# The state-space layer of a decoder trunk: from one scan over 256 tokens to chunks of 8

## The chip, the cores and the metric

One core of a Trainium2 chip runs the whole program. The metric is the device time of one execution in microseconds.

## The reference

Two layers over a residual stream x of 256 tokens by 1024 channels, fp32. Each layer is a gated FFN (1024 to 2816 and back), a mixing step, and a second FFN. The mixing step projects the normalised x by one matrix `w_in` and feeds three mixers: sparse attention (A), a state-space layer (B) and dilated attention (C). Each result goes through its own matrix, is gated by a sigmoid, and the sum goes through `w_out`.

The state-space layer has 32 groups of 16 channels, each with 64 complex states and a diagonal transition:

```
lam_bar = exp(lam * dt);  b_bar = (lam_bar - 1) / lam * b
state[t] = lam_bar * state[t-1] + b_bar @ u[t]
y[t] = Re(c @ state[t]) + d * u[t]
y_b = gelu(y);  y_b = (y_b @ glu_a) * sigmoid(y_b @ glu_b)
```

## The kernel before, in words

Weights are streamed. The list `units` holds them in blocks of 512 KB in the order of use. SP's queue loads each block into one of four buffers `raw` (`load_unit`, line 215); ScalarE rounds it to `wh` (line 226); VectorE, and for a part GpSimd, takes the rest `wl` (lines 230 to 235). Each product is three matmuls in fp32r, high by high and the two cross terms (`mm3`, lines 109 to 111). A block is 24 such matmuls of 256 columns. SP also issues almost every other transfer, in one order.

The Tile framework sets the order on each engine from a simulated timeline and from priorities; `tc.high_priority(offset=-200)` lowers the priority of what is in it.

The FFN (`ffn`, line 341) goes over 11 blocks of 256 hidden channels; in each, VectorE multiplies gate and up, ScalarE rounds (line 375), GpSimd takes the rest (line 376), and the down product follows two blocks later. After each block it calls `side(j)`, into which `step` hangs the set-up of the state-space layer during the first FFN of each layer: `setup_s5_params` once, `setup_s5_layer` one yield at a time, and `setup_s5_table` for each quarter q of the 32 groups.

`setup_s5_table` makes the phase table e^(i theta t) for t = 1 to 256 by eight doublings on GpSimd (lines 493, 495 and 496; VectorE helps at line 494) and stores 1 MB per quarter to DRAM (line 498). `setup_s5_layer` makes the input matrices (to DRAM, as high and low parts) and the output matrices `Cw`, with 16 transposes.

The mixing step is `mix1` (projections, attention, the state-space layer) and `mix2` (GLU, gates, `w_out`). In `mix1` the generator `s5` works on a pair of groups per yield, 16 pairs in a layer. It copies u (high, low, high) into 96 rows of `ub` by twelve small transfers for two pairs (line 825), loads matrix and table (lines 830, 832), multiplies (two matmuls of 256 columns, line 836), turns the product by the table (VectorE line 841, GpSimd 842 and 843), scans the real and the imaginary part over all 256 tokens (line 846), turns back (849 to 851) and multiplies by `Cw` in plain fp32 (line 856). After four pairs come D u and GELU (lines 862 to 870), which leave `yGh` and `yGl` for the GLU.

The order within `mix1` is written by hand: `run(gA, 1)`, `run(gC, n)` and `run(gS, next(steps))` take steps of the attentions and of `s5` between the projections; `SCH` and `steps` say how many for `s5`.

Of the kernel before, what the change touches and what calls it, by code (L numbers as in the profile page):

```python
# [23 lines left out]
F32 = mybir.dt.float32  # L24
# [6 lines left out]
P = 128  # L31
# [11 lines left out]
M_GM, M_CP, M_CN, M_END = 1408, 1410, 1538, 1666  # L43


def const_masks():
# [29 lines left out]
def _body(ctx, tc, nc, I, out, depth, dbg):  # L76
# [119 lines left out]
    YB, VB, MB = 2,4,4  # L196
    DC, BB = V, 1
# [4 lines left out]
    SCH = [1], [2,1,1], [1]  # L202
    TJ = 2
    PO = 100
    TO, TV = -200, 64
# [188 lines left out]
    par = sb([P, 5, 32], F32, "par")  # L394
    smT = sb([P, 16], F32, "smT")
    gqk = sb([P, 4], F32, "gqk")

    def setup_small():
        st = tb([16, P], F32, "st_small")
# [3 lines left out]
        nc.sync.dma_start(st[8:16, :], I["s5_d"].rearrange("l (q g) c -> (l q) (g c)", g=8))  # L403
        pt = ps("y")
        PE.transpose(pt[:, :16], st, ident[:16, :16])
        V.tensor_copy(smT, pt[:, :16])
        V.tensor_tensor(gqk[:, 0:2], smT[:, 0:2], smT[:, 2:4], op=ALU.mult)
        V.tensor_tensor(gqk[:, 2:4], smT[:, 4:6], smT[:, 6:8], op=ALU.mult)

    def setup_s5_params():  # L410
        n = 32
# [23 lines left out]
        V.tensor_copy(im, pt[:, n:2 * n])  # L435
# [4 lines left out]
        r, k = par[:, 0], t("k")  # L440
# [13 lines left out]
        sn, cs = par[:, 4], par[:, 3]  # L454
# [5 lines left out]
        nr, ni, den = t("nr"), t("ni"), t("den")  # L460
        V.tensor_tensor(nr, r, cs, op=ALU.mult)
        V.tensor_scalar(nr, nr, -1.0, None, op0=ALU.add)
# [5 lines left out]
        fr, fi = par[:, 1], par[:, 2]  # L468
# [7 lines left out]
        V.tensor_tensor(fi, fi, den, op=ALU.mult)  # L476

    td = dram.tile([P, 4, 8 * SEQ], F32, name="td", tag="td")
    xd = [dram.tile([P, D], F32, name=f"xd{t}", tag=f"xd{t}") for t in range(2)]
    Bd = [dram.tile([P, 4, 2, P], F32, name=f"Bd{p}", tag=f"Bd{p}") for p in "hl"]  # L480
    Cw = [sb([P, 4, P], F32, f"Cw{i}") for i in range(2)]

    def setup_s5_table(l, q):
        with tc.high_priority(offset=TO):
            tab = tb([P, 4, 2, SEQ], F32, "tab", 1)
            for i in range(2):
                G.tensor_copy(tab[:, :, i, 0], par[:, 3 + i, 16 * l + 4 * q:16 * l + 4 * q + 4])
            n = 1
            while n < SEQ:
                a = tab[:, :, :, 0:n]  # L490
                m = [tb([P, 4, 2, SEQ // 2], F32, f"s5m{i}") for i in range(2)]
                cn, sn = (tab[:, :, i, n - 1:n].unsqueeze(2).broadcast_to([P, 4, 2, n]) for i in range(2))
                G.tensor_tensor(m[0][:, :, :, :n], a, cn, op=ALU.mult)  # L493
                (V if n >= TV else G).tensor_tensor(m[1][:, :, :, :n], a, sn, op=ALU.mult)
                G.tensor_tensor(tab[:, :, 0, n:2 * n], m[0][:, :, 0, :n], m[1][:, :, 1, :n], op=ALU.subtract)  # L495
                G.tensor_tensor(tab[:, :, 1, n:2 * n], m[0][:, :, 1, :n], m[1][:, :, 0, :n], op=ALU.add)  # L496
                n *= 2
            nc.sync.dma_start(td[:, q], tab.rearrange("p j i t -> p (j i t)"))

# [589 lines left out]
```

## Time and profile before

| what | value |
| --- | --- |
| median of 3 runs | 1398.12 us (1396.41 to 1398.65) |
| the profiled execution | 1397.8 us |
| its span, first to last instruction | 1396.0 us |
| mean granted TensorE clock | 0.985 |
| TensorE busy | 1334.4 us, 96% |
| VectorE busy | 948.0 us, 68% |
| ScalarE busy | 670.4 us, 48% |
| GpSimd busy | 639.8 us, 46% |
| DMA | 255.86 MB, mean 183 GB/s |

The busy shares are means over stages that differ: the FFNs, the FFNs with set-up beside them, and the mixing steps. A granted clock of 1 is 2.4 GHz, 0.5 is 1.2 GHz. Matmuls are pipelined: the duration of one record is longer than the distance to the next.

### The profile page before, as it was taken

What the parts mean: (1) busy time and instruction counts of PE and PEld (TensorE: products, weight loads), DVE (VectorE), ACT (ScalarE), POOL (GpSimd) and SP (SyncE); (2) the same over time, 40 slices, a digit from 0 to 9 for tenths busy, and PEclk for the clock granted to TensorE, in tenths of its full rate; (3) what the DMA queues carried; (4) which work ended last, traced back from release to release, by engine and by line L of the source; (5) the groups of instructions that cost most, each with busy time, mean ns of one, the idle gap of its engine ahead of it and who ended that gap; (6) DMA issues with size and microseconds to landing.
All of it is one profiled execution on the core that took longest, in us unless ns stands there. A gap on an engine that the chain in (4) does not pass through costs nothing.

```text
span 1396.0 us, 24668 instructions
## 1 busy us (share of the span) xinstructions
PE 1334.4 (96%) x9624; PEld 1230.7 (88%) x9624; DVE 948.0 (68%) x1256; ACT 670.4 (48%) x962; POOL 639.8 (46%) x670
## 2 busy tenths in 40 slices
PE   8998999988999999999999989999899999999998
PEld 7987899977789989999998889899787899899997
DVE  5656666999997475444667565579999955744443
ACT  5442355656454545444543334466655545544442
POOL 0678705476667441111178751165766765211110
PEclk9999999999999999999999999999999999999999
DMA  8755587555446656666755667755544475466662
GB/s 260 229 181 170 183 273 221 154 151 151 139 132 201 191 175 196 182 182 185 233 164 185 215 207 227 232 176 155 166 141 131 139 222 186 133 213 184 186 190 91
DMA packets 210388, 255.86 MB, mean 183 GB/s; under 512 B 22552, under 2 KB 190560, under 8 KB 209248
## 3 DMA queue, kind: packets, MB, share of 16 engines
q1 hardware_dynamic: 209552, 251.67, 59.1%
q10 hardware_dynamic: 720, 2.62, 0.5%
q8 instruction: 75, 1.23, 0.4%
q14 instruction: 41, 0.34, 0.1%
HBM read 237.48 MB, written 13.63 MB: 180 GB/s over the span
## 4 chain that ended last, share of the span: by engine, by line
PE 60%; POOL 16%; DVE 13%; DMA 6%; issue 4%; ACT 1%; SPq 0%; POOLq 0%; ACTq 0%; DVEq 0%
PE mm L111 14%; PE mm L110 14%; PE mm L109 14%; POOL s5m L493 4%; POOL tab L495 3%; DVE wl L233 3%; POOL tab L496 2%; DMA td<-tab 2%; PE pt L110 2%; PE pt L111 2%; PE pt L109 2%; PE sc L111 2%; PE sc L110 2%; PE sc L109 2%; DMA raw<-in_ffn_gate_dram 2%
## 5 line engine op out<-in xcount | busy, mean ns | idle before, releaser
L233 DVE TENSOR_TENSOR wl<-raw,wh 128x1024 fp32r<-128x1024 f32 (+3 forms) x376 | 487.5, 1304 | 266.6 <-ACT wh L226 263.5
L226 ACT ACTIVATE wh<-raw 128x1024 fp32r<-128x1024 f32 (+2 forms) x396 | 413.1, 1047 | 436.7 <-PE mm L110 197.4
L111 PE MATMUL mm<-hTh,wl 128*128 128x256 f32 x1728 | 495.3, 287 | 12.8 <-DVE wl L233 12.7
L110 PE MATMUL mm<-hTl,wh 128*128 128x256 f32 x1728 | 492.7, 285 | 0.0
L109 PE MATMUL mm<-hTh,wh 128*128 128x256 f32 x1728 | 492.6, 285 | 0.0
L111 PEld LDWEIGHTS mm<-hTh,wl 128*128 128x128 f32 x1728 | 329.2, 191 | 17.5 <-DVE wl L233 14.9
L109 PEld LDWEIGHTS mm<-hTh,wh 128*128 128x128 f32 x1728 | 330.1, 191 | 4.1 <-issue 3.2
L110 PEld LDWEIGHTS mm<-hTl,wh 128*128 128x128 f32 x1728 | 328.8, 190 | 4.6 <-issue 3.6
L376 POOL TENSOR_TENSOR al<-aa,ah 128x512 fp32r<-128x512 f32 x40 | 71.6, 1791 | 427.7 <-ACT ah L375 409.9
L235 POOL TENSOR_TENSOR wl<-raw,wh 128x384 fp32r<-128x384 f32 (+2 forms) x108 | 135.5, 1260 | 34.9 <-ACT wh L226 31.0
L109 PE MATMUL mm<-wh,hTh 128*128 128x256 f32 (+1 forms) x496 | 142.4, 289 | 1.1 <-DVE yGl L710 0.9
L110 PE MATMUL mm<-wl,hTh 128*128 128x256 f32 (+1 forms) x496 | 142.3, 289 | 0.0
L111 PE MATMUL mm<-wh,hTl 128*128 128x256 f32 (+1 forms) x496 | 140.3, 287 | 0.0
L110 PEld LDWEIGHTS mm<-wl,hTh 128*128 128x128 f32 x496 | 94.0, 190 | 3.1 <-issue 2.5
L109 PEld LDWEIGHTS mm<-wh,hTh 128*128 128x128 f32 x496 | 94.1, 190 | 2.9 <-PE mm L111 1.2
L111 PEld LDWEIGHTS mm<-wh,hTl 128*128 128x128 f32 x496 | 93.3, 190 | 1.5 <-issue 0.8
L230 POOL TENSOR_TENSOR wl<-raw,wh 128x512 fp32r<-128x512 f32 x40 | 56.6, 1435 | 49.5 <-ACT wh L226 49.5
L846 DVE TENSOR_TENSOR_SCAN v<-par,v 128x256 f32<-128x256 f32 x64 | 61.8, 971 | 3.7 <-POOL v L842 3.5
L110 PE MATMUL pt<-wl,ah 128*128 128x512 f32 x144 | 57.1, 397 | 5.7 <-DVE wl L233 5.7
L493 POOL TENSOR_TENSOR s5m<-tab 128x8 f32<-128x8 f32 (+3 forms) x64 | 55.8, 872 | 4.7
L850 POOL TENSOR_TENSOR v<-M 128x256 f32<-128x256 f32 x32 | 26.0, 812 | 68.7 <-DVE M L849 61.0
L111 PE MATMUL pt<-wh,al 128*128 128x512 f32 x144 | 56.7, 393 | 0.0
(288 smaller groups left out, 2288.5 us busy)
## 6 DMA issues: line engine op xcount, KB each, us to landing
raw<-in_w_in_dram SPq DMA_DIRECT2D x100, 512.0 KB
raw<-in_ffn_gate_dram SPq DMA_DIRECT2D x88, 512.0 KB
raw<-in_ffn_up_dram SPq DMA_DIRECT2D x88, 512.0 KB
raw<-in_ffn_down_dram SPq DMA_DIRECT2D x88, 512.0 KB
td<-tab SPq DMA_DIRECT2D x8, 1024.0 KB
tab<-td SPq DMA_DIRECT2D x16, 512.0 KB
raw<-in_w_out_dram SPq DMA_DIRECT2D x16, 512.0 KB
raw<-in_w_branch_a_dram SPq DMA_DIRECT2D x8, 512.0 KB
```

The source lines that it names most:

```text
L109: PE.matmul(o, lh, rh, start=start, stop=False)
L110: PE.matmul(o, lh, rl, start=False, stop=False)
L111: PE.matmul(o, ll, rh, start=False, stop=stop)
L226: A.activation(hv, r, AF.Copy)
L230: G.tensor_tensor(lv[:, :, cs], r[:, :, cs], hv[:, :, cs].bitcast(F32), op=ALU.subtract)
L233: V.tensor_tensor(lv[:, :, :c], r[:, :, :c], hv[:, :, :c].bitcast(F32), op=ALU.subtract)
L235: G.tensor_tensor(lv[:, :, c:], r[:, :, c:], hv[:, :, c:].bitcast(F32), op=ALU.subtract)
L376: G.tensor_tensor(al, a, ah.bitcast(F32), op=ALU.subtract)
L493: G.tensor_tensor(m[0][:, :, :, :n], a, cn, op=ALU.mult)
L495: G.tensor_tensor(tab[:, :, 0, n:2 * n], m[0][:, :, 0, :n], m[1][:, :, 1, :n], op=ALU.subtract)
L496: G.tensor_tensor(tab[:, :, 1, n:2 * n], m[0][:, :, 1, :n], m[1][:, :, 0, :n], op=ALU.add)
L846: V.tensor_tensor_scan(v[:, i], rr, v[:, i], 0.0, op0=ALU.mult, op1=ALU.add)
```

## The change

The state-space layer is reformulated by chunks of 8 tokens (32 chunks). Within a chunk the output is a lower triangular block Toeplitz matrix of 8 x 16 by 8 x 16 per group, times the chunk's 128 inputs; a second 128x128 matrix takes the inputs to the state at the chunk's end, a third takes the state before the chunk to the outputs. States of 64 complex numbers lie as 128 partitions (real and imaginary halves). Only the step between chunks is scanned: 32 steps for each of the 8 groups of a quarter, all in one instruction of 256 elements, whose factor is zero where a group begins.

Set-up: `setup_s5_params` keeps lam_bar and its second and fourth power, the phase of the eighth, and its modulus. `setup_s5_layer` makes eight powers `Qt` on VectorE, one phase table of 32 steps for all groups on GpSimd, and per quarter the matrices F (GpSimd) and H (VectorE), 128x1024 each. F is transposed (8 transposes) and stored to `Ad`; H is stored to `Gd`; the Toeplitz blocks are 16 short matmuls of F by H, stored to `Kd`. All of it is inside the lowered priority.

Run time: u is stored to DRAM with its tokens reversed in each chunk, and read back with (channel, token) on the partitions; the result goes to DRAM in the same way and comes back as `yGh` and `yGl`, whose tokens are then ordered by place in the chunk first. The GLU's last two steps in `mix2` write them back to token order by a strided view. All matmuls of the new layer are in plain fp32: per quarter 8 in `enter` and 16 in `leave`, with 32 columns each.

```diff
-    SCH = [1], [2,1,1], [1]
...
-    def setup_s5_table(l, q):
...
-            while n < SEQ:
...
-            nc.sync.dma_start(td[:, q], tab.rearrange("p j i t -> p (j i t)"))
...
+        for i, nme in enumerate(("s5_b_re", "s5_b_im")):
+            nc.sync.dma_start(b[0][64 * i:64 * i + 64], I[nme][l].rearrange("g p c -> p g c"))
+            nc.sync.dma_start(b[1][64 - 64 * i:128 - 64 * i], b[0][64 * i:64 * i + 64])
...
+        Qt = tb([P, 2, 2, 32, 8], F32, "s5Q")
...
+        while n < 32:
+            mm = [a[:, :64 * n].rearrange("p (a g n) -> p a g n", a=2, n=n) for a in m]
             for i in range(2):
+                G.tensor_tensor(mm[i], tab[:, :, :, :n], tab[:, i, :, n - 1:n].unsqueeze(1).broadcast_to([P, 2, 32, n]), op=ALU.mult)
+            G.tensor_tensor(tab[:, 0, :, n:2 * n], mm[0][:, 0], mm[1][:, 1], op=ALU.subtract)
+            G.tensor_tensor(tab[:, 1, :, n:2 * n], mm[0][:, 1], mm[1][:, 0], op=ALU.add)
+            n *= 2
...
+        for i, a in enumerate((tab[:, 0], tab[:, 1], R)):
+            nc.sync.dma_start(td[:, :, i, :], a.rearrange("p (q g) k -> p q (g k)", q=4))
...
+        for q in range(4):
+            gs = slice(8 * q, 8 * q + 8)
+            F, m1 = xt(0), xt(1)
+            f4, m4 = (a.rearrange("p (g c n) -> p g c n", g=8, n=8) for a in (F, m1))
+            for i, o in enumerate((f4, m4)):
+                G.tensor_tensor(o, b[i][:, gs].unsqueeze(3).broadcast_to([P, 8, 16, 8]),
+                                Qt[:, i, 1, gs].unsqueeze(2).broadcast_to([P, 8, 16, 8]), op=ALU.mult)
+            G.tensor_tensor(F, F, m1, op=ALU.add)
+            H, m2 = xt(0), xt(1)
...
+            V.tensor_tensor(H, H, m2, op=ALU.add)
+            nc.sync.dma_start(Gd[:, q], H)
             yield
+            At = xt(1)
+            for hf in range(2):
+                pt = ps("y")
+                for g in range(4):
+                    k = 4 * hf + g
+                    PE.transpose(pt[:, g * P:(g + 1) * P], F[:, k * P:(k + 1) * P], ident)
+                A.activation(At[:, 512 * hf:512 * hf + 512], pt, AF.Copy)
+            nc.sync.dma_start(Ad[:, q], At)
+            pk = ps("y")
+            for s in range(2):
+                for part in range(2):
+                    for a in range(4):
+                        g = 4 * s + a
+                        o = pk[32 * a:32 * a + 32, 128 * s:128 * s + 128]
+                        lh = F[:, (g - a % 2) * P:(g - a % 2 + 2) * P:8]
+                        if part:
+                            PE.matmul(o[:, 16:], lh, h4[:, g, 0:7].rearrange("p n c -> p (n c)"), start=True, stop=True)
...
+            for a in range(4):
+                nc.sync.dma_start(Kd.rearrange("(s a) x n c -> a x s (n c)", a=4)[a][:, 2 * q:2 * q + 2, 112:],
...
-            A.activation(uh, pu, AF.Copy)
-            V.tensor_tensor(ul, pu, uh.bitcast(F32), op=ALU.subtract)
+            uv = tb([P, 512], F32, "M", MB).rearrange("p (c t) -> p c t", c=2)
+            A.activation(uv.rearrange("p c (r k) -> p c r k", r=8), pu.rearrange("p c (k r) -> p c r k", r=8)[:, :, ::-1, :], AF.Copy)
+            nc.sync.dma_start(ud[2 * b:2 * b + 2].rearrange("q p t -> p q t"), uv)
...
+            def late(q):
+                Gt, Tt = tb([P, 8, 128], F32, "s5G"), tb([P, 8, 128], F32, "s5T")
+                nc.sync.dma_start(Gt.rearrange("p g e -> p (g e)"), Gd[:, q])
+                kq = Kd[8 * q:8 * q + 8]
+                for r in range(8):
+                    nc.sync.dma_start(Tt[r::8], kq[:, :, r:r + 8, :].rearrange("g x n c -> x g (n c)"))
...
+            def enter(q):
+                At = sb([P, 1024], F32, "x0")
+                nc.sync.dma_start(At, Ad[:, q])
+                tab = tb([P, 3, 256], F32, "tab")
+                nc.sync.dma_start(tab, td[:, q])
+                U = tb([P, 8, 32], F32, "s5U", 2)
+                nc.sync.dma_start(U, ud[q].rearrange("(g c) (r k) -> (c r) g k", c=16, r=8))
+                bu = ps("p2")
+                for g in range(8):
+                    PE.matmul(bu[:, 32 * g:32 * g + 32], At[:, P * g:P * g + P], U[:, g], start=True, stop=True)
+                X = bu[:, :256]
+                sw = tb([P, 256], F32, "s5sw")
+                for e in range(2):
+                    A.activation(sw[hps[e]], X[hps[1 - e]], AF.Copy)
+                v, w = tb([P, 256], F32, "s5v", 2), tb([P, 256], F32, "s5w", 2)
+                V.tensor_tensor(v, X, tab[:, 0], op=ALU.mult)
+                V.tensor_tensor(w, sw, tab[:, 1], op=ALU.mult)
+                V.tensor_tensor(v, v, w, op=ALU.subtract)
+                V.tensor_tensor_scan(v, tab[:, 2], v, 0.0, op0=ALU.mult, op1=ALU.add)
...
+            def leave(q, Gt, Tt):
+                U, v = st.pop(q)
                 yT = ps("y")
+                for g in range(8):
+                    PE.matmul(yT[:, 32 * g:32 * g + 32], Tt[:, g], U[:, g], start=g == 0, stop=False)
+                for g in range(8):
+                    PE.matmul(yT[:, 32 * g + 1:32 * g + 32], Gt[:, g], v[:, 32 * g:32 * g + 31], start=False, stop=g == 7)
...
+                for r in range(8):
+                    nc.sync.dma_start(yd[q].rearrange("i (g c) (r k) -> r c (i g) k", c=16, r=8)[r],
+                                      yo[16 * r:16 * r + 16].bitcast(F32).rearrange("p i (g k) -> p (i g) k", k=32))
+
+            def back(q):
+                for i, a in enumerate((yGh, yGl)):
+                    nc.sync.dma_start(a[:, q].bitcast(F32), yd[q, i])
...
+        steps = iter([1, 0, 1, 0, 1, 0] + [1, 0, 1] + [1, 0, 1, 0, 1, 0, 1, 0] + [1] * 4)
```

## Rows read from the trace of the kernel before

**Rows 1.** The page, part 1: busy us, share of the span, instructions.

```profile
PE 1334.4 (96%) x9624; PEld 1230.7 (88%) x9624; DVE 948.0 (68%) x1256; ACT 670.4 (48%) x962; POOL 639.8 (46%) x670
```

**Rows 2.** Windows by stage: us, busy us of each engine (instructions), clock, DMA share, GB/s.

```profile
15.00:222.40 207.40, 197.33 (x1348) 183.13 (x1347) 132.40 (x145) 87.70 (x105) 113.52 (x151) 0.97 0.69 214
222.40:517.70 295.30, 278.19 (x2112) 252.19 (x2111) 248.08 (x412) 161.38 (x273) 188.24 (x169) 0.99 0.56 167
517.70:706.50 188.80, 188.80 (x1342) 178.04 (x1342) 97.44 (x94) 86.76 (x102) 19.21 (x12) 1.00 0.63 189
706.50:909.10 202.60, 194.01 (x1357) 181.59 (x1356) 126.17 (x107) 85.65 (x103) 110.63 (x150) 0.98 0.65 206
909.10:1205.20 296.10, 278.94 (x2112) 253.13 (x2111) 248.92 (x411) 161.63 (x273) 188.23 (x169) 0.99 0.55 167
1205.20:1393.00 187.80, 187.09 (x1326) 176.04 (x1324) 88.78 (x84) 78.55 (x89) 18.14 (x11) 1.00 0.54 164
```

**Rows 3.** Windows within the mixing stage of layer 0, columns as above.

```profile
245.00:280.00 35.00, 33.96 (x284) 33.51 (x283) 34.39 (x98) 22.80 (x44) 16.83 (x15) 1.00 0.54 151
280.00:315.00 35.00, 28.92 (x218) 25.34 (x217) 34.65 (x57) 20.44 (x40) 27.39 (x25) 1.00 0.51 147
240.00:445.00 205.00, 189.41 (x1495) 169.04 (x1494) 194.37 (x349) 114.28 (x209) 137.48 (x130) 0.98 0.52 152
```

**Rows 4.** Groups by line, 240 to 445 us: count, busy us, mean ns, idle before.

```profile
L846 DVE TENSOR_TENSOR_SCAN v<-par,v 128x256 f32<-128x256 f32 x32 | 30.5, 959 | 1.8 <-POOL v L842 1.7
...
L849 DVE TENSOR_TENSOR M<-v,tab 128x512 f32<-128x512 f32 x32 | 23.3, 768 | 0.1
L841 DVE TENSOR_TENSOR M<-p,tab 128x512 f32<-128x512 f32 x32 | 20.9, 680 | 0.2
...
L634 ACT ACTIVATE cq<-pt 64x512 fp32r<-64x512 f32 x6 | 3.5, 588 | 11.2 <-DVE cq L635 11.2
...
L740 DVE TENSOR_TENSOR yAl<-pt,yAh 128x256 fp32r<-128x256 f32 x2 | 0.8, 408 | 0.0
```

**Rows 5.** Groups by line on PE, mixing stage of layer 0, columns as above.

```profile
L109 PE MATMUL mm<-hTh,wh 128*128 128x256 f32 x224 | 64.2, 287 | 0.0
...
L856 PE MATMUL y<-v,Cw 128*32 128x256 f32 x64 | 15.8, 414 | 7.3 <-POOL v L850 7.3
...
L836 PE MATMUL p<-x,bs 96*128 96x256 f32 x32 | 7.4, 313 | 3.0 <-issue 3.0
```

**Rows 6.** Timeline of PE and its weight loads: start, duration, what, count.

```profile
358.20 0.28 PE L109 MATMUL mm<-hTh,wh 128*128 128x256 f32 x1
358.32 0.28 PE L110 MATMUL mm<-hTl,wh 128*128 128x256 f32 x1
...
360.31 0.28 PE L774 MATMUL sc<-ck,cq 128*128 128x128 f32 x1
360.42 0.28 PE L775 MATMUL sc<-ckl,cq 128*128 128x128 f32 x1
...
400.87 1.53 PE L788 MATMUL pt<-att_pt,cv 128*64 128x128 f32 x24
...
402.33 0.20 PEld L734 LDWEIGHTS pt<-ident,att_s 128*128 128x128 f32 x2 [0.17 <-ACT att_s L722]
```

**Rows 7.** Groups by line, 705 to 925 us, the set-up's and the FFN's.

```profile
L376 POOL TENSOR_TENSOR al<-aa,ah 128x512 fp32r<-128x512 f32 x10 | 18.1, 1806 | 65.8 <-ACT ah L375 48.0 <-DMA raw<-in_w_in_dram 17.8
...
L493 POOL TENSOR_TENSOR s5m<-tab 128x1024 f32<-128x1024 f32 x4 | 11.8, 2944 | 0.3
...
L494 DVE TENSOR_TENSOR s5m<-tab 128x1024 f32<-128x1024 f32 x4 | 4.9, 1226 | 4.0 <-POOL tab L496 4.0
```

**Rows 8.** The chain that ended last, near 84 us: start, us, what.

```profile
84.41 7.82 DMA td<-tab
```

**Rows 9.** Line 825's issues on SP: ns min/median/max, first and last start.

```profile
L825 SPq DMA_DIRECT2D x<-yGh x64: 507/581/1439, 255.3 to 1076.1; - x64
```

**Rows 10.** The page, part 3: queue, packets, MB, share of 16 engines.

```profile
q1 hardware_dynamic: 209552, 251.67, 59.1%
```

More of the change, by code (lines that the diff above doesn't have):

```diff
@@ L402, in setup_small @@
                 nc.sync.dma_start(st[2 * i:2 * i + 2, 64 * hf:64 * hf + 64], I[nme])
-        nc.sync.dma_start(st[8:16, :], I["s5_d"].rearrange("l (q g) c -> (l q) (g c)", g=8))
         pt = ps("y")
-        PE.transpose(pt[:, :16], st, ident[:16, :16])
-        V.tensor_copy(smT, pt[:, :16])
+        PE.transpose(pt[:, :8], st, ident[:8, :8])
+        V.tensor_copy(smT, pt[:, :8])
+        for i in range(2):
+            V.tensor_tensor(sgn[:, i:i + 1], cm[:, M_GM + 1 - i:M_GM + 2 - i], cm[:, M_GM + i:M_GM + i + 1], op=ALU.subtract)
         V.tensor_tensor(gqk[:, 0:2], smT[:, 0:2], smT[:, 2:4], op=ALU.mult)
@@ L459, in setup_s5_params @@
         A.activation(cs, k, AF.Sin)
[L460 to L462 removed]
+        nr, den = t("nr"), t("den")
+        ni = zs[:, 0, 1, 0]
+        V.tensor_tensor(zs[:, 0, 0, 0], r, cs, op=ALU.mult)
+        V.tensor_scalar(nr, zs[:, 0, 0, 0], -1.0, None, op0=ALU.add)
         V.tensor_tensor(ni, r, sn, op=ALU.mult)
@@ new lines, in setup_s5_params @@
+        sq = tb([P, 2, 2, n], F32, "sp_sq")
+        for i in range(3):
+            a, b = zs[:, i], zs[:, i + 1]
+            V.tensor_tensor(sq, a, a, op=ALU.mult)
+            V.tensor_tensor(b[:, 0], sq[:, 0], sq[:, 1], op=ALU.subtract)
+            V.scalar_tensor_tensor(b[:, 1], a[:, 0], 2.0, a[:, 1], op0=ALU.mult, op1=ALU.mult)
+        V.tensor_copy(lam, zs[:, 0:3, :, 0])
+        V.tensor_copy(u8, zs[:, 3, :, 1])
+        V.tensor_tensor(r8, r, r, op=ALU.mult)
+        V.tensor_tensor(r8, r8, r8, op=ALU.mult)
@@ new lines, in s5 @@
+            st = {}
+            def late(q):
[4 more added lines that the diff above has]
+                    nc.sync.dma_start(Tt[r::8], kq[:, :, r:r + 8, :].rearrange("g x n c -> x g (n c)"))
+                return Gt, Tt
+            def enter(q):
[17 more added lines that the diff above has]
+                V.tensor_tensor_scan(v, tab[:, 2], v, 0.0, op0=ALU.mult, op1=ALU.add)
+                sw = tb([P, 256], F32, "s5sw")
+                for e in range(2):
+                    A.activation(sw[hps[e]], v[hps[1 - e]], AF.Copy)
+                V.tensor_tensor(v, v, tab[:, 0], op=ALU.mult)
+                V.tensor_tensor(w, sw, tab[:, 1], op=ALU.mult)
+                V.tensor_tensor(v, v, w, op=ALU.add)
+                st[q] = U, v
@@ L873, in run @@
+            GT = late(0)
+            for q in range(5):
+                if q < 4:
+                    enter(q)
+                    yield
+                if q > 0:
+                    leave(q - 1, *GT)
+                    if q < 4:
+                        GT = late(q)
+                    if q > 1:
+                        back(q - 2)
+                    yield
+            back(3)
         def run(gen, n=None):
@@ L884, in mix1 @@
         gS = s5()
-        steps = iter([v for a, k in zip(SCH, (6, 3, 8)) for v in (a * k)[:k]] + [1] * 4)
+        steps = iter([1, 0, 1, 0, 1, 0] + [1, 0, 1] + [1, 0, 1, 0, 1, 0, 1, 0] + [1] * 4)
         for g in range(3):
@@ L1007, in f @@
                         setup_s5_params()
-                next(gen, None)
-                if j % TJ == 0 and (j - 2) // TJ < 4:
-                    setup_s5_table(l, (j - 2) // TJ)
+                with tc.high_priority(offset=TO):
+                    next(gen, None)
         return f
```

234 lines of the change are left out of this document (98 added, 136 removed).

## The prediction, made before the changed kernel was built or run

> **What bounds the kernel now.** I read the page's busy shares first, then a table by stage, then the stretch that differs. TensorE is busy for 1334 of 1396 us [rows 1], so the time can fall only by TensorE's idle time, by its half-speed stretches, or by work taken off it. The stage table [rows 2] cuts the span at the last update of x in each stage (line 329). The second FFN of layer 0 shows the pace of weights alone: 188.8 us, no idle time, full clock. The FFN of layer 1 with the state-space set-up beside it takes 202.6 us, 13.8 more for the same weights. The two mixing stages take 295.3 and 296.1 us; TensorE is busy for 278.2 of the first, so 17.1 us are idle, and the granted clock of 0.99 says that some of it ran at 1.2 and not 2.4 GHz. A mean of 0.99 costs about 1% of the stage, 3 us.
>
> Why TensorE idles there shows in the slices [rows 3]: from 245 to 315 us VectorE is busy for 34.4 and 34.7 of every 35 us while TensorE drops to 28.9. VectorE is full, and everything TensorE waits for (the transposed operands, the softmax minima) stands in its line. So VectorE sets the pace of that stretch and TensorE the rest.
>
> **What leaves VectorE.** One layer's rows [rows 4]: 32 scans of 256 (30.5 us), 32 products after them (23.3) and 32 before them (20.9), together 74.7 us of VectorE's 194.4 in that stretch. The new code has 4 chunks, each with one scan of the same 256 elements (0.96 us) and six products or sums of 128x256. The nearest row for such a one is the 128x256 subtract, 0.41 us: 0.96 + 6 x 0.41 = 3.4 us, 13.7 per layer. GELU's steps change little (two additions with D go, one product comes from GpSimd) and I leave them even. Net 61 us per layer leave an engine that had 10 us to spare; it then has about 133 us of work in 205. All of GpSimd's additions on v go too. ScalarE gets four half-partition copies per chunk, at most 0.59 us each (line 634 copies twice the width [rows 4]), some 9 us in a stage where it is busy for 161 of 295 [rows 2]; covered.
>
> **What changes on TensorE in a mixing stage.** Out go 64 output products (15.8 us) and 32 input products (7.4): 23.2 us, and with them 7.3 + 3.0 us of idle time right before them [rows 5]. In come 24 matmuls a chunk, 96 a layer: plain fp32, a full 128x128 stationary block, 32 moving columns. The trace has none like it, so bounds. Below: 24 matmuls of line 788 (fp32, half-width weights, in pairs) in 1.53 us, 0.064 each. Above: 0.41 us, the whole duration of an fp32 matmul of 256 columns at line 856, as if nothing overlapped. Between them lie 4-byte 128x128 weights under 128 columns, which start 0.11 us apart at lines 774 and 775 [rows 6]; the weights, not the columns, must set that pace, since 256 columns start 0.12 us apart. Plain fp32 may load worse, so I take 0.14: 96 x 0.14 = 13.4 us.
>
> Of the old idle time and lost clock, 17.1 + 3.0 = 20.1 us, I let 5 us stay: waits on the attention's own chains (normalise, transpose, softmax), which are late next. Gain per mixing stage: 23.2 + 15.1 - 13.4 = 24.9 us, two layers 49.8.
>
> A rule that speaks against this: the Trainium skill, "FP8 and Floating Point Precision", TensorE Precision Notes, counts four passes through the array for true fp32. The trace neither proves nor excludes it here: the fp32 matmul of line 856 lasts 0.414 us where a one-pass one of the same 256 columns lasts 0.287 [rows 5], more than one pass and less than four. If weights were loaded for each pass, the price would go to the upper bound; that is a rival below.
>
> **The set-up, beside the first FFN of each layer.** Out go the tables: 8 doubling steps per quarter on GpSimd, the longest 2.9 us an instruction, between which the FFN's own 1.8 us subtract (line 376) has to stand in line, and a table store whose landing (7.82 us) holds GpSimd's next table [rows 7, 8]. In come one table of 32 steps (the same kinds of instruction, five doublings, no second table waiting for a store) and per quarter three GpSimd and three VectorE operations on 128x1024. On VectorE these cost 12 x 1.23 = 15 us per layer, plus about 6 for the eight powers, less 4.9 or more of its share in the tables [rows 7]; it is busy for 126 of 202.6 us [rows 2], so they are covered. What is not covered is TensorE's: 24 transposes more (40 for 16; the pair at 402.33 loads in 0.20, so 0.10 each [rows 6]: 2.4 us) and 64 short matmuls for the Toeplitz blocks at 0.064 (4.1 us): 6.5 us per layer. Against it stand the old stalls: 13.8 us in layer 1, and in layer 0 10.1 idle plus 3% of clock (6.2): 16.3. I let 5 us of stalls stay in each, because the two transposed halves and the Toeplitz blocks of each quarter pass one after the other through the one PSUM bank "y": twelve hand-overs from TensorE to ScalarE and back per layer. Gain: 13.8 - 11.5 = 2.3 and 16.3 - 11.5 = 4.8, together 7.1.
>
> **DMAs and the queue of SP.** Each mixing stage issues 90 transfers for this layer in place of 80, the set-up 40 in place of 14. At the 0.58 us of the old small copies [rows 9] that is 21 us more of SP's time over 500 us; SP mostly waits for a free weight buffer, so nothing. By the row of q1 [rows 10] a packet takes 0.591 x 16 x 1396 / 209552 = 63 ns on average, at 1.2 KB. The new layouts move 24,600 runs of 128 bytes; at no less than nothing and at most 63 ns each they add up to 97 us of all 16 engines over two stages of 591, from a share of 0.55 to 0.71 [rows 2]. Hidden either way. What matters is the order: SP also issues the weight loads, and a load that reads what a store wrote waits in SP for the landing. Four weight buffers of 24 matmuls at 0.12 us (lines 109 and 110 [rows 6]) are 11.5 us of cover.
>
> The strided copies (u reversed, the merge back to token order) have no row; nothing below, and above as much again as a 128x256 operation, 8 x 0.41 = 3 us in all, under other matmuls. I take nothing.
>
> **Sum.** 49.8 + 7.1 = 56.9 us off the profiled 1397.8 (span 1396.0 and 1.8 around it; the median of the runs is 1398.12, the same): **1341 us**.
>
> **Rivals.**
> 1. Everything waiting goes and the short matmuls run at 0.064: mix 23.2 + 20.1 - 6.1 = 37.2 each, set-up 30.1 - 13 = 17.1, together 91.5: 1306 us. For it: VectorE is the only full engine. Against: softmax chains need TensorE, VectorE and ScalarE in turn.
> 2. The old waits before the state-space matmuls come back as waits for their loads (u and y go out to DRAM and return): 10.3 us a stage stay beside the 5, and the set-up gains nothing. 23.2 + 4.8 - 13.4 = 14.6 a stage: 1369 us. For it: TensorE takes its work in order, and the 3.0 us before line 836 were already of that kind.
> 3. The 192 short matmuls of both layers cost 0.41 each: 192 x 0.27 = 52 us more than in the sum, 1393 us. That is what the four passes of the Trainium skill (same section) would come to if each pass also reloads the weights.
> 4. **Slower: SP blocks the weights.** A chunk has two places where a load waits for a store (u, y), 8 a layer. If each holds SP for two landings in a row as long as the table store's, 2 x 7.82 = 15.6 us, the 11.5 us of weight buffers run dry and TensorE stands still for 4.1 us, 16 times: 66 us, 1407 us. It decides from holds of 11.5 + 56.9/16 = 15 us. For it: one queue for everything. Against: that store is 1 MB, and the new ones are 256 KB.
>
> **How the numbers follow.** Chances: forecast 0.51 (1326 to 1356), rival 1 0.15, rival 2 0.17, rival 3 0.07, rival 4 0.10. A measurement of this kernel tells 0.2%, about 3 us. Forecast and rivals 1 and 2 are faster, rival 3 by a hair and with half its chance surely: 0.86 faster, 0.03 the same, 0.11 slower. The range goes from a little under rival 1 to just short of rival 3: 1297 to 1390; what is left out is most of rivals 3 and 4 and a little below.
>
> **What would show each step.** Right: scans at 8 and not 64, VectorE at 70 to 80% in the mixing stages and below 90% in every slice from 245 to 385; mixing stages of 265 to 275 us; the 192 short matmuls starting 0.10 to 0.16 us apart; the FFN with set-up within 12 us of the one without. Wrong: TensorE idle before the short matmuls with a DMA as releaser (rival 2), starts 0.3 us or more apart (rival 3), weight conversions on ScalarE waiting for a raw load in the mixing stage (rival 4), or clock levels of 0.9 where it is 1.0 now.

## The result, and the profile of the changed kernel

The changed kernel takes 1364.13 us (median of 4 runs, 1362.91 to 1365.29) where the kernel before, on the same chip, takes 1398.38: a ratio of 0.9756 with an interval of 0.9739 to 0.9772. It is faster, as forecast, and inside the range; but it gained 34 us where 57 were forecast.

The page's busy shares and the row of SP's queue, against [rows 1] and [rows 10]:

```profile
PE 1333.8 (98%) x10120; PEld 1257.6 (92%) x10120; DVE 842.1 (62%) x1166; ACT 700.7 (51%) x1018; POOL 474.4 (35%) x333
...
q1 hardware_dynamic: 245488, 261.44, 64.0%
```

TensorE is busy for as long as before (1334 us): what went is idle time, and the matmuls taken out were replaced by as much work. VectorE lost 106 us, GpSimd 165.

The table by stage, cut as in [rows 2] (us, busy us of PE, PEld, DVE, ACT and POOL with their instructions, clock, DMA share, GB/s):

```profile
15.00:219.00 204.00, 198.89 (x1501) 183.25 (x1500) 153.71 (x180) 94.84 (x117) 91.69 (x50) 1.00 0.73 224
219.00:504.50 285.50, 277.96 (x2207) 266.66 (x2206) 177.01 (x337) 169.37 (x289) 132.45 (x101) 0.98 0.64 186
504.50:693.20 188.70, 188.70 (x1342) 177.98 (x1341) 97.27 (x94) 86.89 (x102) 19.21 (x12) 1.00 0.64 188
693.20:893.50 200.30, 197.53 (x1508) 184.21 (x1507) 140.67 (x126) 92.82 (x115) 77.63 (x49) 1.00 0.68 214
893.50:1171.70 278.20, 273.40 (x2209) 262.62 (x2208) 178.40 (x339) 169.50 (x289) 133.04 (x101) 1.00 0.65 191
```

Beside [rows 2]: the FFNs with set-up went from 207.4 to 204.0 and from 202.6 to 200.3, the FFN without set-up stands at 188.7. The mixing stages went from 295.3 to 285.5 and from 296.1 to 278.2: 9.8 and 17.9 us, where the forecast had 24.9 for each. The two layers run the same code and differ by 7.3 us; that is the first question. Why even the better one is 7 us short is the second.

The matmul groups of the mixing stage of layer 0, against [rows 5]:

```profile
L900 PE MATMUL p<-s5U,x 128*128 128x32 f32 x64 | 9.4, 304 | 2.5 <-DMA s5U<-ud 2.5
...
L922 PE MATMUL y<-s5U,s5T 128*128 128x32 f32 x64 | 8.1, 268 | 0.0
L924 PE MATMUL y<-s5v,s5G 128*128 128x31 f32 x64 | 7.8, 275 | 0.0
...
L637 PE MATMUL pt<-ident,qn 128*128 128x128 f32 x32 | 5.3, 283 | 2.9 <-DVE qn L633 2.9
```

The code issues 32 matmuls on each of lines 900, 922 and 924 (4 chunks of 8). The trace has 64 of each. A plain fp32 matmul is two records, each with its own weight load: 192 in the stage, not 96. The timeline of PE gives their pace:

```profile
297.65 1.42 PE L922 MATMUL y<-s5U,s5T 128*128 128x32 f32 x12
298.90 1.95 PE L924 MATMUL y<-s5v,s5G 128*128 128x31 f32 x16
300.69 0.37 PE L106 MATMUL mm<-wh,hTh 128*128 128x256 f32 x1
...
352.50 3.62 PE L900 MATMUL p<-s5U,x 128*128 128x32 f32 x16 [2.49 <-DMA s5U<-ud]
```

Sixteen records of line 924 stand between 298.90 and 300.69: 0.112 us each, close to the 0.11 and 0.12 us of 128x128 weights under 128 and 256 columns [rows 6]. The last row is as many records of line 900 at 352.50, after a wait of 2.49 us for the load of u; the next matmul starts at 355.94, so these take 0.215 us each. Windows around both places, columns as in the stage table:

```profile
297.00:301.00 4.00, 4.00 (x37) 3.98 (x37) 3.09 (x7) 2.90 (x5) 2.83 (x2) 1.00 0.78 248
301.00:304.40 3.40, 3.40 (x18) 3.07 (x16) 3.25 (x6) 0.64 (x2) 0.33 (x2) 0.50 0.53 142
304.40:308.00 3.60, 3.60 (x31) 3.29 (x32) 2.88 (x12) 2.29 (x6) 1.53 (x1) 1.00 0.97 310
350.00:352.50 2.50, 0.01 (x1) 0.00 (x0) 1.91 (x4) 1.53 (x5) 1.00 (x1) 0.93 0.52 85
352.50:359.00 6.50, 6.50 (x30) 6.50 (x31) 1.45 (x4) 1.26 (x3) 0.00 (x0) 0.50 0.86 280
```

The granted clock is 0.50, that is 1.2 GHz, in two stretches of 9.9 us together. A short record takes 0.215 us there and 0.112 at 2.4 GHz; if all the work in them slows down alike, half of the time is lost, an estimate of 5.0 us. One follows the wait for u. The other follows the short matmuls, with TensorE busy for all of the 4 us ahead of it. The chain of waits around the wait for u (start, us, what):

```profile
342.13 5.43 DMA s5G<-Gd
...
347.93 0.45 SPq L936
...
349.93 2.53 DMA s5U<-ud
...
352.50 3.62 PE p L900 x16
```

The load of u is issued by SP behind the y stores (line 936), which in this chain follow the load of G. SP's own rows show that its order differs between the layers (first two rows layer 0, last two the same quarter in layer 1):

```profile
345.27 4.61 SPq L936 DMA_DIRECT2D yd<-s5y  x8
349.93 0.46 SPq L897 DMA_DIRECT2D s5U<-ud  x1
...
1018.13 0.59 SPq L897 DMA_DIRECT2D s5U<-ud  x1
1018.82 5.18 SPq L936 DMA_DIRECT2D yd<-s5y  x8
```

In layer 1 the load stands ahead of the stores, and TensorE does not wait for it.

Last the slices, against [rows 3]:

```profile
240.00:275.00 35.00, 32.96 (x275) 32.15 (x274) 33.55 (x103) 23.44 (x48) 14.79 (x14) 1.00 0.65 185
275.00:310.00 35.00, 34.08 (x278) 32.84 (x278) 31.36 (x64) 27.93 (x60) 17.85 (x14) 0.95 0.67 192
310.00:345.00 35.00, 35.00 (x304) 33.41 (x302) 22.40 (x44) 26.03 (x48) 12.71 (x9) 1.00 0.63 181
```

VectorE is still full in the first 35 us (the attention's own work and 7.9 us of weight rests; the state-space lines 906 to 909 take 1.9), and by the third slice it has room (22.4 of 35). The DMAs carry 36,000 packets more, and TensorE waits for none of them but that one load of u.

### The profile page after: what moved, and what is told of

The parts are those of the page before. It is cut to its first block, busy times and chain, and to the rows that moved or that the text cites. A ratio compares the mean times of both kernels' runs of the same rounds, so it can differ in the third digit from the quotient of the medians.

```text
span 1362.7 us, 25418 instructions
## 1 busy us (share of the span) xinstructions
PE 1333.8 (98%) x10120; PEld 1257.6 (92%) x10120; DVE 842.1 (62%) x1166; ACT 700.7 (51%) x1018; POOL 474.4 (35%) x333
## 4 chain that ended last, share of the span: by engine, by line
PE 76%; DVE 8%; DMA 6%; POOL 5%; ACT 2%; issue 2%; SPq 1%; POOLq 0%; ACTq 0%; DVEq 0%
PE mm L108 18%; PE mm L106 17%; PE mm L107 17%; DVE wl L228 3%; PE pt L108 3%; PE pt L107 3%; PE pt L106 3%; PE sc L108 2%; PE sc L107 2%; PE sc L106 2%; DMA raw<-in_w_in_dram 2%; DMA raw<-in_ffn_gate_dram 1%; ACT wh L221 1%; DMA raw<-in_ffn_down_dram 1%; PE p L900 1%
## 5 line engine op out<-in xcount | busy, mean ns | idle before, releaser
L228 DVE TENSOR_TENSOR wl<-raw,wh 128x1024 fp32r<-128x1024 f32 (+3 forms) x376 | 471.8, 1262 | 338.2 <-ACT wh L221 334.0
L106 PEld LDWEIGHTS mm<-hTh,wh 128*128 128x128 f32 x1728 | 326.6, 189 | 2.2
L107 PEld LDWEIGHTS mm<-hTl,wh 128*128 128x128 f32 x1728 | 325.2, 188 | 1.6 <-issue 0.3
L371 POOL TENSOR_TENSOR al<-aa,ah 128x512 fp32r<-128x512 f32 x40 | 68.2, 1706 | 466.1 <-ACT ah L370 466.1
L230 POOL TENSOR_TENSOR wl<-raw,wh 128x384 fp32r<-128x384 f32 (+2 forms) x108 | 144.9, 1347 | 199.6 <-ACT wh L221 166.9
L108 PE MATMUL sc<-wh,al 128*128 128x512 f32 x144 | 56.5, 392 | 0.0
L106 PE MATMUL pt<-wh,ah 128*128 128x512 f32 x144 | 56.4, 392 | 0.0
L107 PE MATMUL sc<-wl,ah 128*128 128x512 f32 x144 | 56.3, 391 | 0.0
```

The costliest lines, as they stand in the source:

```text
L106: PE.matmul(o, lh, rh, start=start, stop=False)
L107: PE.matmul(o, lh, rl, start=False, stop=False)
L108: PE.matmul(o, ll, rh, start=False, stop=stop)
L228: V.tensor_tensor(lv[:, :, :c], r[:, :, :c], hv[:, :, :c].bitcast(F32), op=ALU.subtract)
L230: G.tensor_tensor(lv[:, :, c:], r[:, :, c:], hv[:, :, c:].bitcast(F32), op=ALU.subtract)
L371: G.tensor_tensor(al, a, ah.bitcast(F32), op=ALU.subtract)
```

## The experiments

The theory after the result: VectorE's line did set the old pace and no longer does; what is missing is the doubled count of short matmuls, and in layer 0 the wait for u with the slow clock behind it. The edits below are against the changed kernel, except three that are against the kernel before. Stage times are those of the one profiled execution of each run.

**The short matmuls in fp32r.** A, T and u are declared as the reduced-precision type of four bytes; G stays plain.

```diff
-                At = sb([P, 1024], F32, "x0")
+                At = sb([P, 1024], F32R, "x0")
...
-                U = tb([P, 8, 32], F32, "s5U", 2)
+                U = tb([P, 8, 32], F32R, "s5U", 2)
...
-                Gt, Tt = tb([P, 8, 128], F32, "s5G"), tb([P, 8, 128], F32, "s5T")
+                Gt, Tt = tb([P, 8, 128], F32, "s5G"), tb([P, 8, 128], F32R, "s5T")
```

> Blocks A and T and the input u of the state-space layer are declared fp32r in place of plain fp32, so these products run in reduced precision; the products with G stay plain fp32. Theory (the miss is the price of plain fp32: the trace of after has two records per matmul, 0.112 us apart, so 192 and not 96 per layer): lines 900 and 922 fall from 128 to 64 records each, their distance stays near 0.11 us, 64 x 0.112 = 7.2 us per mixing stage, 14 us in all: about 1350 us. Rival (the short matmuls wait in the shadow of other stalls, or fp32r loads cost twice as much): under 4 us, 1360 or more.

Measured: 1355.48 us (1354.33 to 1358.52), ratio 0.9696 (0.9668 to 0.9724). Its PE groups in the mixing stage of layer 0, and its two mixing stages:

```profile
L924 PE MATMUL y<-s5v,s5G 128*128 128x31 f32 x64 | 9.4, 293 | 0.0
L637 PE MATMUL pt<-ident,qn 128*128 128x128 f32 x32 | 5.3, 283 | 4.6 <-DVE qn L633 4.6
L922 PE MATMUL y<-s5U,s5T 128*128 128x32 f32 x32 | 4.4, 255 | 0.0
L900 PE MATMUL p<-s5U,x 128*128 128x32 f32 x32 | 4.1, 256 | 0.0
```

```profile
220.70:496.90 276.20, 269.22 (x2144) 258.83 (x2143) 181.06 (x339) 168.80 (x289) 132.03 (x101) 0.99 0.67 192
...
885.80:1161.30 275.50, 269.20 (x2144) 258.80 (x2143) 182.61 (x339) 168.95 (x289) 132.69 (x101) 0.99 0.67 193
```

The records of lines 900 and 922 halve, those of line 924, left plain, don't: the type sets the count. The gain is 8.6 us, less than the 14 expected and more than the rival's 4. Part of the time came back as waits for the normalised q (line 637 waits 4.6 us and not 2.9) and as clock (0.99 in layer 1, where it was 1.00). The 9.3 us of layer 0 are not the price of the records alone, since its wait for u is gone too; in layer 1, which had no such wait, 64 records fewer took 4.2 us off TensorE's busy time and 2.7 off the stage.

**u from another queue.** The load of u is issued by ScalarE's queue.

```diff
-                nc.sync.dma_start(U, ud[q].rearrange("(g c) (r k) -> (c r) g k", c=16, r=8))
+                nc.scalar.dma_start(U, ud[q].rearrange("(g c) (r k) -> (c r) g k", c=16, r=8))
```

> Only the load of u (256 KB per quarter) is issued from ScalarE's queue and not from SP's. Theory (in layer 0 TensorE waits 2.5 us for this load, which stood in SP behind nine loads of G and T and eight stores of y; the wait drops TensorE's clock for 6.8 us, 3.4 us lost): the wait and the 1.2 GHz stretch behind it go, the mixing stage of layer 0 falls by 5 to 7 us to about 279, layer 1 stays at 278: about 1358 us. Rival (the order of ScalarE is disturbed by the waits of the issue, or the next load in SP is late instead): mixing stage of layer 0 at 284 to 287, no gain or a loss of a few us.

Measured: 1361.69 us (1361.08 to 1362.64), ratio 0.9734 (0.9712 to 0.9756). The two mixing stages, and two windows between:

```profile
221.70:500.20 278.50, 274.39 (x2211) 264.37 (x2210) 178.43 (x338) 169.42 (x289) 131.94 (x101) 0.99 0.66 190
...
890.00:1169.70 279.70, 274.44 (x2208) 264.03 (x2207) 179.71 (x339) 169.32 (x289) 133.01 (x101) 0.99 0.66 190
...
266.40:269.90 3.50, 3.50 (x35) 3.50 (x33) 3.43 (x15) 3.31 (x4) 0.65 (x2) 1.00 0.71 186
269.90:273.30 3.40, 3.40 (x18) 3.40 (x18) 3.33 (x18) 1.61 (x8) 0.75 (x1) 0.50 0.61 172
```

Layer 0 loses its wait and 7.0 us, nearly all that set it apart from layer 1. But layer 1 takes 1.5 us more, and the two FFNs with set-up 3.5, at clocks of 0.98 to 0.99 where they were 1.00. The last two rows show one such stretch, in layer 0, with TensorE busy throughout. So the total falls by 2.4 us and not by 6, and the intervals of the two ratios overlap (0.9712 to 0.9756 and 0.9739 to 0.9772).

**The floor.** The run-time part of the state-space layer is left out (no loads, matmuls, scans, GELU), and u goes straight to the GLU; the set-up stays.

```diff
-        gS = s5()
+        gS = iter(range(8))
```

> Leaves out the run-time part of the state-space layer: u goes straight to the GLU, no loads, no short matmuls, no scan; the set-up stays. It gives the floor of a mixing stage. Theory (in layer 1 nothing but the 192 records of 0.112 us is left of the layer's cost): the mixing stages fall from 285 and 278 to 256 to 258 us each. Rival (the attention's chains share waits with it, so more goes than TensorE's own time): 245 to 252. Rival (the layer runs in gaps that stay without it): 265 or more.

Measured: 1321.28 us (one run). The mixing stages:

```profile
219.30:480.00 260.70, 254.59 (x2016) 243.42 (x2015) 164.51 (x296) 157.15 (x261) 136.47 (x101) 0.99 0.55 161
...
869.10:1128.70 259.60, 254.17 (x2016) 243.34 (x2015) 164.74 (x296) 157.33 (x261) 136.31 (x101) 0.99 0.55 162
```

The floor keeps 5.4 to 6.1 us idle. The old layer cost 34.6 and 36.5 us above it, the new one 24.8 and 18.6; 192 records at 0.112 are 21.5. In layer 1 TensorE's busy time falls by 19.2 us (273.4 to 254.2), and the floor has a stretch of 3.4 us at 1.2 GHz in each stage, by estimate 1.7 us of lost clock, which explains most of what is missing to 21.5. The stages lie 1.6 to 2.7 us above the theory's 256 to 258; neither rival came.

**VectorE filled up again.** 160 products of 128x240 a stage that nobody reads.

```diff
+            def load(n):
+                for i in range(n):
+                    V.tensor_tensor(dum, dum, dum, op=ALU.mult)
...
+                load(20)
```

> Adds 40 multiplications of 128x240 on a scratch tile to VectorE per quarter, 20 after the scan and 20 within GELU: 160 x 0.39 = 62 us per mixing stage, what the change took off VectorE. Theory (VectorE set the pace of the old mixing stage): the stages lengthen by 12 to 25 us each, to 290 to 303, with VectorE above 95% for over 100 us again. Rival (the gain came from TensorE's own work and from GpSimd's additions, VectorE had only followed): under 5 us each.

Measured: 1380.42 us (one run). The added products took 74 us in layer 0, more than planned, and VectorE's busy time as a whole rose by 64. Slices and mixing stages:

```profile
245.00:280.00 35.00, 33.05 (x275) 32.20 (x273) 34.46 (x89) 18.00 (x30) 15.24 (x11) 1.00 0.62 171
280.00:315.00 35.00, 32.58 (x257) 31.61 (x258) 34.56 (x101) 28.62 (x66) 16.49 (x14) 0.95 0.70 190
...
220.60:510.70 290.10, 278.74 (x2208) 266.59 (x2207) 241.42 (x500) 167.25 (x289) 126.43 (x101) 0.98 0.65 183
...
899.80:1187.50 287.70, 281.50 (x2208) 270.16 (x2207) 242.21 (x499) 167.95 (x289) 126.42 (x101) 0.97 0.66 185
```

VectorE is as full as it was before (34.6 of 35, [rows 3]; over 97% from 240 to 390 us), yet the stages are only 4.6 and 9.5 us longer: layer 0 at the rival's end, layer 1 between the two. In this run TensorE never waits for u, so for layer 0 the fairer base is the 278.5 us with u moved, and the difference 11.6. Either way it is less than the theory's 12 to 25 and, but for the first base, more than the rival's 5. Full is not the same as late; in the second slice TensorE is busy for 32.6 us, and in the old kernel for 28.9. What else the old line had, products and sums that the output matmuls wait for, the next three runs take out.

**Three cuts in the old kernel.** Before the output matmuls it turned the states back: two products of 128x512 on VectorE and two sums on GpSimd, 16 times a layer. The first cut leaves out all of it, the second the sums, the third the products.

```diff
-                    M = [tb([P, 512], F32, "M", MB).rearrange("p (i t) -> p i t", i=2) for _ in range(2)]
-                    for i in range(2):
-                        V.tensor_tensor(M[i], v, tj[i], op=ALU.mult)
-                    G.tensor_tensor(v[:, 0], M[0][:, 0], M[0][:, 1], op=ALU.subtract)
-                    G.tensor_tensor(v[:, 1], M[1][:, 0], M[1][:, 1], op=ALU.add)
```

> The kernel before, leaving out the turning back of the scanned state (lines 849 to 851): 23 us less on VectorE and 25 us less on GpSimd per mixing stage, nothing less on TensorE. Theory as it now stands (a full VectorE costs little by itself; the old stage paid for TensorE's own 23 us and the waits before lines 836 and 856, 10 us): 3 to 8 us per stage, 1382 to 1392. Rival (the prediction's: VectorE set the pace): 12 us or more per stage, under 1374.

Measured: 1369.19 us (one run).

```profile
225.40:504.90 279.50, 273.79 (x2112) 250.04 (x2111) 218.46 (x380) 160.97 (x273) 160.11 (x137) 1.00 0.59 177
...
896.60:1176.20 279.60, 273.45 (x2112) 249.93 (x2111) 219.22 (x380) 160.98 (x273) 161.88 (x137) 1.00 0.60 177
```

The stages lose 15.8 and 16.5 us: in layer 0 idle time falls from 17.1 to 5.7, and the clock is 1.00. That is well above the 3 to 8 of the theory that VectorE's load counts for little. The other two cuts take the sums and the products one at a time; their rows are those of layer 0.

The second cut puts in the place of these five lines

```diff
+                    M = tb([P, 512], F32, "M", MB).rearrange("p (i t) -> p i t", i=2)
+                    V.tensor_tensor(M, v, tj[1], op=ALU.mult)
+                    V.tensor_tensor(v, v, tj[0], op=ALU.mult)
```

> The kernel before, leaving out GpSimd's two sums of the turning back (lines 850 and 851); VectorE does both products (line 849), the second in place. It takes 25 us of GpSimd and one hand-over off each mixing stage and leaves VectorE's load. Leaving out products and sums together gave 16 us per stage. Theory (the old stage paid for the hand-over to GpSimd, on which TensorE's next work waits): 10 us or more per stage, mixing stages at 286 or less, the time under 1380. Rival (VectorE's load paid): under 5 us per stage, 1390 or more.

Measured without the sums: 1385.62 us, ratio 0.9907 (0.9892 to 0.9921).

```profile
222.90:511.40 288.50, 273.95 (x2112) 252.73 (x2111) 242.11 (x411) 160.83 (x273) 159.99 (x137) 0.99 0.58 171
```

and the third

```diff
+                    G.tensor_tensor(v[:, 0], v[:, 0], v[:, 1], op=ALU.subtract)
+                    G.tensor_tensor(v[:, 1], v[:, 1], v[:, 0], op=ALU.add)
```

> The kernel before, leaving out VectorE's two products of the turning back (line 849), 23 us per mixing stage; GpSimd still does its two sums, on the scanned state itself, and TensorE still waits for them. Theory (hand-over to GpSimd): under 6 us per stage, 1386 or more. Rival (VectorE's load): 10 us or more per stage, under 1380.

Measured without the products: 1375.28 us, ratio 0.9835 (0.982 to 0.985).

```profile
222.70:506.80 284.10, 274.83 (x2112) 250.26 (x2111) 226.11 (x379) 161.77 (x273) 188.99 (x169) 1.00 0.59 174
```

The sums alone are worth 6.8 us, the products 11.2, both 15.8. My theory that the step by GpSimd was the larger share fell, and so did its rival of under 5 us for the sums. The products are 22.0 us of VectorE (248.1 to 226.1) and gave 11.2 us of time. The sums are GpSimd's, yet without them VectorE's busy time fell by 6.0 us as well (to 242.1) and the stage by 6.8. So the 15.8 us for 29.6 us off VectorE with both out are not the worth of its load alone: each cut also shortens the chain that line 856 waits for, and no run takes load off VectorE and leaves that chain as it was. With both out the idle time is down to that of the floor. The other 41 us that the change takes off VectorE bought next to nothing more: without the turn-back the old layer 1 takes 279.6 us, with as much work on TensorE (273.5) as the changed layer 1 (273.4), which takes 278.2.

**The set-up of layer 1 left out**, so that its tables are those of layer 0.

```diff
-            gs = setup_s5_layer(l)
+            gs = setup_s5_layer(l) if l == 0 else iter(())
```

> Layer 1 uses the matrices that layer 0 made; its set-up is left out, the rest stays. The prediction has 6.5 us of TensorE work and 5 us of stalls per set-up. Theory: the first FFN of layer 1 falls from 200.3 to 188.8 us, the time by 11 to 12 to 1352. Rival (the second FFN is no fair measure for the first, whose end and projections differ): a fall of under 8 us.

Measured: 1355.88 us (one run). The FFN of layer 1:

```profile
691.80:880.60 188.80, 188.80 (x1340) 178.03 (x1340) 95.91 (x94) 85.28 (x101) 21.66 (x14) 1.00 0.63 189
```

188.8 instead of 200.3: the set-up costs 11.5 us. The whole gained less, 8.3 us, and missed the 1352, since the mixing stage of layer 1 then took 282.7 us with a clock of 0.98. In this run SP issues the load of u behind the y stores in layer 1 too, and TensorE waits 1.3 us for it there (2.3 in layer 0).

**All three groups in fp32r**, G with 32 columns (a zero column ahead), u from ScalarE's queue. v and w have one buffer each and not two.

```diff
-                Gt, Tt = tb([P, 8, 128], F32, "s5G"), tb([P, 8, 128], F32, "s5T")
+                Gt, Tt = tb([P, 8, 128], F32R, "s5G"), tb([P, 8, 128], F32R, "s5T")
...
-                    PE.matmul(yT[:, 32 * g + 1:32 * g + 32], Gt[:, g], v[:, 32 * g:32 * g + 31], start=False, stop=g == 7)
+                    PE.matmul(yT[:, 32 * g:32 * g + 32], Gt[:, g], v[:, g], start=False, stop=g == 7)
```

> All short matmuls of the state-space layer in fp32r (reduced precision), those with G on 32 columns with a zero first column, and the load of u from ScalarE's queue. Theory (records count): 96 records in place of 192 per mixing stage at 0.112 us, 10.8 us less than with the load of u alone moved, whose run gave 1361.7: 1340 us, mixing stages near 268. Rival (the run with A and T in fp32r gave 4 us per stage and not 7, since TensorE then waits for VectorE and the clock drops): 1346 to 1352.

Measured: 1349.68 us (1349.09 to 1350.24), ratio 0.9653 (0.9636 to 0.9671), and a window of layer 0:

```profile
218.90:494.70 275.80, 268.08 (x2112) 256.35 (x2111) 181.45 (x339) 168.46 (x289) 130.81 (x105) 0.98 0.66 193
...
884.50:1156.50 272.00, 263.40 (x2112) 252.13 (x2111) 181.82 (x338) 168.31 (x289) 131.67 (x105) 1.00 0.67 195
...
297.20:307.50 10.30, 9.62 (x46) 9.62 (x47) 8.29 (x14) 3.23 (x7) 4.46 (x5) 0.50 0.83 236
```

In layer 1, where the clock is 1.00 in both kernels, 96 records fewer (2209 to 2112 in the rows, one of them at the window's edge) took 10.0 us off TensorE's busy time (273.4 to 263.4): 0.104 each, close to the 0.112 of the timeline. Of these 10.0 only 6.2 reached the stage: 3.8 are idle time now, 2.2 of them before line 637, which waits 4.8 us and not 2.6 for the normalised q. Layer 0 has 10.3 us at 1.2 GHz. So the rival (1346 to 1352) held, not the 1340.

**T and G in two steps**, with other work between them, so that no 32 short records stand in a row; u from ScalarE's queue. The list `steps` gives `s5` four more steps.

```diff
+                yield
...
-                    leave(q - 1, *GT)
+                    yield from leave(q - 1, *GT)
```

> The 8 matmuls with T and the 8 with G of a quarter are taken in two steps with other work between, and the load of u comes from ScalarE's queue. Theory (a block of short matmuls without any wait is followed by a stretch at 1.2 GHz: 3.3 us of lines 714 and 900 at 266 us and 2.8 us of lines 922 and 924 at 1035 in the run with the load of u moved): shorter blocks, at most one such stretch left in the mixing stages, 2 to 4 us less than 1361.7. Rival (the stretches have another cause, or the scheduler puts the halves together again): within 2 us of 1361.7.

Measured: 1360.1 us (1357.78 to 1360.87), ratio 0.9724 (0.9707 to 0.9741).

```profile
219.40:498.70 279.30, 273.97 (x2208) 262.56 (x2207) 178.44 (x338) 168.47 (x289) 134.02 (x101) 1.00 0.66 190
...
888.70:1167.30 278.60, 273.27 (x2208) 262.79 (x2207) 181.28 (x339) 168.83 (x289) 133.29 (x101) 1.00 0.66 190
```

The clock is 1.00 in both stages, and their sum (557.9) is that with u moved alone (558.2). The stretches at 1.2 GHz went and the stages stayed as long: TensorE's busy time fell by 0.4 and 1.2 us, and its idle time rose from 4.1 to 5.3 in layer 0. Such a stretch can cost less than its length says, when waits follow it. The time is 1.6 us below the 1361.7, so the rival held.

**Both together**: fp32r, u moved, two steps.

> All short matmuls in fp32r, the load of u from ScalarE's queue, and the matmuls with T and G in two steps. Theory (the 10 us at 1.2 GHz in layer 0 of the run without the two steps cost 5 us, and shorter blocks avoid them): mixing stages near 271, 1344 to 1347. Rival (TensorE's waits for the normalise chain set the stage whatever the order): within 2 us of 1349.7.

Measured: 1346.67 us (1345.67 to 1349.06), ratio 0.9634 (0.9618 to 0.965); mixing stages of 272.4 and 271.1 us. Time and stages are those of the theory, but its reason held only in part: layer 0 still has 6.8 us at 1.2 GHz (the row is shown at the end). It is faster than both kernels, by the reduced precision of the short matmuls; from the one without the two steps the intervals don't tell it apart.

## Why the prediction was right in direction and 23 us too high in gain

- **What bounds the kernel: right in the main.** VectorE's line set the old pace: without its two products, and with TensorE's 2112 records as they were, the stage fell by 11.2 us, with GpSimd's sums out as well by 15.8. How much of this is VectorE's load and how much the shorter chain before line 856 is not shown. VectorE lost 71 us a stage where 61 were forecast, in part because GELU's steps, which I left even, take 6.3 us in place of 12.1. Its share is 62 and 64%, below the 70 to 80 I gave as a sign, and the first slice is 96% and not below 90. Neither matters: the idle time was down to the floor's after 30 us.
- **The short matmuls: the step that failed.** "96 x 0.14 = 13.4 us" should be 192 x 0.112 = 21.5: 8.1 us too little in each stage, 16.2 of the 23. Taken out again, such records were worth 0.104 us each in TensorE's busy time. The pace was nearly right and the count was not: I counted matmuls in the code and took their price from records. [rows 5] and [rows 6] already had it: 64 records of line 856 for 32 matmuls, 24 of line 788 for 12. The 0.414 us of line 856, which the prediction weighed against passes, is the duration of one of the two records. The same miscount is in the set-up: 168 records beyond the plain FFN's 1340, for 104 transposes and matmuls, of which the 64 plain fp32 matmuls count twice.
- **The idle time that stays: right in layer 1, wrong in layer 0.** I let 5 us stay. Layer 1 has 4.8 with a clock of 1.00. Layer 0 has 7.5 and, by the estimate above, 5.0 of lost clock, 7.5 too much. The two terms give 8.1 + 7.5 = 15.6 for layer 0, where the stage is 15.1 above its forecast of 270.4, and 8.1 - 0.2 = 7.9 for layer 1, where it is 7.0 above 271.2: the sum holds within 1 us a stage.
- **Rival 1 did not come**: 4.8 us of waits stay even in layer 1, and 5.4 to 6.1 in the floor.
- **Rival 2 came true once.** One of the eight loads of u made TensorE wait, 2.5 us, with a DMA as releaser. With nothing but the loads of u moved to another queue, the wait was gone and the stage 7.0 us shorter, clock included. TensorE never waited for a y load.
- **Rival 3 did not.** The records start 0.112 apart and not 0.41. The trace shows two records with two weight loads where the four-byte reduced type shows one. The Trainium skill, "FP8 and Floating Point Precision", TensorE Precision Notes, counts four passes for true fp32. What passes go on inside a record no run here shows. By the Trainium skill, "TensorE: Matmul & The Clock Gate", LDWEIGHTS (loading the stationary operand), a weight load's time goes with its columns, an estimate of 107 ns for 128 of them. The distance of 112 ns from record to record agrees; the profile's own weight-load records, 192 ns long in the median at lines 900 and 922, overlap, so the load by itself is not shown.
- **The set-up: right in layer 1, by luck.** Forecast 11.5 us a layer, measured 11.5 by leaving it out; of it 8.7 are TensorE's work (197.5 against 188.8) and 2.8 stalls, where I had 6.5 and 5: two misses of 2.2 that cancel. In layer 0 the FFN with set-up is 15.2 us above the 188.8. The gain was 3.4 + 2.3 = 5.7 us for 7.1.
- **Rival 4 did not come**: SP waited at most 3.5 us in a row for a y store to land, not 15.6, and TensorE waited for no weight load. ScalarE's conversions wait for raw loads 12.4 and 7.4 us in the mixing stages; before the change it was 11.1 and 12.4. The DMA share rose from 0.56 to 0.64 in layer 0, hidden, within the bounds of 0.55 to 0.71.

Sum: 9.8 + 17.9 + 3.4 + 2.3 = 33.4 us; the two spans (1396.0 and 1362.7) differ by 33.3.

That TensorE waits for u in layer 0 and not in layer 1 goes with SP's order: the load stands behind eight y stores in the one and ahead of them in the other. Without the set-up of layer 1 it stood behind the stores there too, and TensorE waited. It does not always: with A and T in fp32r the load stood behind the stores in both layers, and TensorE waited in neither. Left open is why the same program text gets two orders on SP.

## What to carry to other kernels

Before you price many small matmuls, count the records that one of them makes in a trace, by type: here plain fp32 made two and fp32r one, and a record of 32 columns took 0.11 us, as long as one of 128. An engine that is full costs only what TensorE's next work waits for in its line: the first 30 us taken off VectorE, with GpSimd's sums, gave 16 us, the next 41 next to nothing, and 74 us of unrelated products put back cost 5 to 12. A load that TensorE waits for is better not queued behind stores: moving it took 7.0 us off one stage here, though only 2.4 off the whole.

## What the runs showed of the chip that was not expected

TensorE's clock fell to 1.2 GHz while the engine was busy and waited for nothing: at 301.0 to 304.4 us of the changed kernel, right behind 32 short records, and at 269.9 to 273.3 us with u moved, behind 16 records of line 714 (128 columns) and 16 of line 900 (32 columns). It did not in layer 1 of the changed kernel, with the same records, so they alone don't decide it. With T and G in two steps both mixing stages show 1.00, but with fp32r besides, layer 0 has 6.8 us of it again (first row below), and the floor, which has no short record at all, has 3.4 us in each stage (second row, layer 0). These stretches follow a wait of TensorE: 2.0 us until 298.7 for the normalised q (line 633), and in the floor 2.1 us until 309.4 and until 958.2 for a step of ScalarE (line 630).

```profile
299.50:306.30 6.80, 6.80 (x36) 6.80 (x35) 5.87 (x11) 3.81 (x7) 3.13 (x4) 0.51 0.79 221
...
309.80:313.20 3.40, 3.40 (x19) 3.40 (x18) 3.10 (x5) 2.79 (x5) 1.21 (x2) 0.51 0.48 149
```

The four runs with u moved have mean clocks of 0.990 to 0.995, so the share of slow stretches also changes from one execution to the next.
